# A decoder block's kernel: convolution taps one chunk later, the state space's whole turns rounded by ScalarE, one product by rstd squared, and the last scaling four rows at a time on two engines

## The chip, the cores and the metric

The kernel runs on one core of a Trainium2 chip. The metric is device time in microseconds for one execution, the median of a few runs. Engines are named as the profile names them: PE is TensorE, DVE VectorE, ACT ScalarE, POOL GpSimd, SP the engine that only issues DMAs.

## The reference

One decoder block over 512 tokens of width 2048, batch 1, float32 throughout:

```
proj = rmsnorm(x) @ w_in                      # u, v, gate_b, gate_c (1024 each), merge_a, merge_b (2048 each)
ya   = gelu(s5_scan(u))                       # 64 groups x 64 complex states, a linear recurrence over the tokens
ya   = (ya * sigmoid(ya @ w_glu)) @ w_ssm_out
yb   = (gate_b * causal_dwconv(gate_c * v)) @ w_conv_out        # 3 taps per channel
h    = x + (sigmoid(merge_a) * ya + sigmoid(merge_b) * yb) @ w_o
a    = rmsnorm(h) @ w_up                      # two halves of 5632
h    = h + (gelu(causal_dwconv(a[:5632])) * a[5632:]) @ w_down
out  = rmsnorm(h)                             # mean over channels, times a gain per channel
```

## The kernel before

Channels lie on the 128 partitions, tokens along the free axis. A float32 product is made of three matmuls in a rounded format: each weight chunk and each input is split into a high part and a low part (`hi`, `lo`), and PE runs hi·hi, hi·lo and lo·hi (lines 167 to 169; 1027 to 1029 for `w_up`).

The work is a flat list of *chunks* (128 output channels by 1024 inputs, 24 matmuls of 512 columns). `run` walks it; after the matmuls of chunk i have been written, `after(i)` writes in this order: the split of chunk i+2 (`prep_to`), the loads ahead, one or two pieces of background work (`bg`), the unit's `hooks`, and the unit's `done` if this was its last chunk. Each engine runs its own instructions in the order in which they were written, and waits at semaphores for the others. A chunk has three buffers, so the split of chunk i+2 can start once PE is through chunk i-1.

The split has two forms. For two chunks in three up to the middle of the merge units ACT writes -raw to `lo` (line 145) and raw to `hi` (146), and a DMA on POOL's queue adds raw to `lo` (147), which leaves the low part. For the others ACT writes `hi` (150) and DVE subtracts (129).

In the first stage the chunks are: u (16 chunks), then eight triples of units v, gate_c, gate_b (chunks 16 to 63), then 32 merge units (chunks 64 to 127). Behind them the state space runs as background work, 32 pairs of groups, in pieces called first, second and third: *third* of step n prepares the angles of pair n (`ssm_phase`: a copy to ACT, line 444; on DVE the angle in turns, 449, its rounding to whole turns by adding and subtracting 12582912, line 451, and the difference, 452) and the two matmuls that feed the scan; *first* of step n+1 writes six products on POOL (`ssm_turn`, lines 98 and 490) and half a scan on DVE (lines 98, 478, 479); *second* takes sine and cosine on ACT (`ssm_trig`, 458 to 460) and the other half of a scan. There is one piece a chunk; every fourth merge unit takes two a chunk.

In a triple, `v_done` copies v from PSUM (617) and multiplies it twice by rstd on POOL; `gc_done` multiplies by gate_c on DVE (the zero-padded tile `zp`), and at once applies three taps (`conv3`: line 610 on ACT, 611 and 612 on DVE) and a product by rstd on POOL (`cv`); `gb_done` multiplies by gate_b.

After `w_down`'s first 12 rows of 128 channels the last four rows are computed as eight units of half the tokens (`ends`), so that the first half's norm and stores overlap the second half's matmuls. `dn_done` adds the residual (1156) and squares (859); `out_store` scales a row by its gain and by the norm (1174, DVE, one row of 256 tokens at a time, 32 in all) and stores two rows a DMA, by turns from SP and ACT (1177). After the last matmul: `out_sums(1)`, rows 8 to 15 of the first half, `out_spread(1)`, sixteen rows of the second half. `SHIFT` places the split weights of the `w_down` units, `ends` too, 48 columns further into their buffers.

Of the kernel before, what the change touches and what calls it, by code (L numbers as in the profile page):

```python
# [8 lines left out]
F32 = mybir.dt.float32  # L9
# [3 lines left out]
ALU = mybir.AluOpType  # L13
# [54 lines left out]
def block_kernel(ctx: ExitStack, tc: tile.TileContext, a: dict):  # L68
# [15 lines left out]
    def V(name, i=None):  # L84
        o, w = VEC[name]
        return vec[:, o:o + w] if i is None else vec[:, o + i:o + i + 1]
# [2 lines left out]
    nc.vector.memset(ones, 1.0)  # L89
    halfpi = const.tile([P, 1], F32, tag="halfpi", name="halfpi")  # L90
    nc.vector.memset(halfpi, math.pi / 2)
    warm = const.tile([P, 1], F32, tag="warm", name="warm")
    nc.scalar.activation(warm, halfpi, AF.Copy)
    rstd = const.tile([P, T], F32, tag="rstd", name="rstd")
# [2 lines left out]
    def mul(o, x, y, eng=nc.vector):  # L97
        eng.tensor_tensor(o, x, y, op=ALU.mult)  # L98
# [119 lines left out]
    def add(*units):  # L218
        for u in units:
            flat.extend((u, c) for c in range(len(u.chunks)))  # L220
# [3 lines left out]
    def kd_chunks(w, n):  # L224
        return [(w[2 * n], 8), (w[2 * n + 1], 8)]
# [26 lines left out]
    def norm_spread(big, cols=slice(0, T)):  # L252
        pb = psm.tile([P, T], F32, tag="mm", name="statb")
        nc.tensor.matmul(pb[:, cols], ones, big[:, cols], start=True, stop=True)
        return pb
# [18 lines left out]
    def st(tag, bufs=1, shape=(P, T), dt=F32):  # L274
        return sp.tile(list(shape), dt, tag=tag, name=tag, bufs=bufs)
# [164 lines left out]
    def ssm_phase(p):  # L440

        br = braw.pop(p)
        bs = st("bst", 3, (P, 2, P), F32R)
        nc.scalar.activation(bs, br, AF.Copy)
        nc.vector.tensor_tensor(bs[64:], br[64:], bs[64:].bitcast(F32), op=ALU.subtract)
        bst[p] = bs
        ph, nk = st("ph", 2), st("nk")
        ph3 = ph.rearrange("p (a b) -> p a b", a=16)
        nc.vector.tensor_tensor(ph3, pha[:, p, :].unsqueeze(2).to_broadcast([P, 16, 32]),
                                phb[:, p, :].unsqueeze(1).to_broadcast([P, 16, 32]), op=ALU.add)  # L450
        nc.vector.tensor_scalar(nk, ph, MAGIC, MAGIC, op0=ALU.add, op1=ALU.subtract)
        nc.vector.tensor_tensor(ph, ph, nk, op=ALU.subtract)
        phs[p] = ph

    def ssm_trig(p):
        ph = phs.pop(p)
        t = pairt("cs", 3)
        nc.scalar.activation(t[:, 1], ph, AF.Sin, scale=TURN)
        nc.scalar.activation(t[:, 0], ph, AF.Abs)
        nc.scalar.activation(t[:, 0], t[:, 0], AF.Sin, scale=-TURN, bias=halfpi)  # L460
        cs[p] = t
# [21 lines left out]
    def ssm_turn(p):  # L483
        t, z = cs.pop(p), zz.pop(p)
        x = pairt("xx", 5)
        for j in range(2):
            w = st("pt")
            mul(x[:, j], z[:, j], t[:, 0], nc.gpsimd)
            mul(w, z[:, 1 - j], t[:, 1], nc.gpsimd)
            nc.gpsimd.tensor_tensor(x[:, j], x[:, j], w, op=ALU.add if j else ALU.subtract)  # L490
        xx[p] = x
# [22 lines left out]
    def bg_pieces(n):  # L514

        def ok(p):
            return 0 <= p < NPAIR

        def quad(m):
            return m % 4 == 3 and ok(m)  # L520

        def first():
            if quad(n - 6):
                ssm_y((n - 6) // 4)
            if quad(n - 5):
                ssm_out((n - 5) // 4)
            if ok(n - 3):
                ssm_turn(n - 3)
            if ok(n - 2):
                ssm_scan(n - 2, 0)  # L530

        def second():
            if ok(n - 1):
                ssm_trig(n - 1)
            if ok(n - 2):
                ssm_scan(n - 2, 1)

        def third():
            if quad(n - 4):
                ur_load((n - 4) // 4)  # L540
            if ok(n - 1):
                ssm_bu(n - 1)
            if ok(n):
                ssm_phase(n)
                ssm_load(n + 1)
        return [first, second, third]
# [43 lines left out]

    def u_first():
        nc.vector.tensor_copy(rstd, norm_spread(big[0]))
        for i in range(4):
            mul(uts[i], uts[i], rstd)

# [12 lines left out]
    def conv3(dst, zp, w, b, i, nw):  # L608

        nc.scalar.activation(dst, zp[:, 2:], AF.Identity, scale=V(w, 2 * nw + i), bias=V(b, i))  # L610
        nc.vector.scalar_tensor_tensor(dst, zp[:, 1:T + 1], V(w, nw + i), dst, op0=ALU.mult, op1=ALU.add)
        nc.vector.scalar_tensor_tensor(dst, zp[:, 0:T], V(w, i), dst, op0=ALU.mult, op1=ALU.add)

    def v_done(i):
        def f(ps):
            hold["v"] = st("mt", 2)
            nc.scalar.activation(hold["v"], ps, AF.Copy)
            mul(hold["v"], hold["v"], rstd, nc.gpsimd)
            mul(hold["v"], hold["v"], rstd, nc.gpsimd)
        return f  # L620

    def gc_done(i):
        def f(ps):
            z = zpad[i % 2]
            mul(z[:, 2:], ps, hold["v"])
            hold["cv"] = st("cv", 2)
            conv3(hold["cv"], z, "cw", "cb", i, KS)
            mul(hold["cv"], hold["cv"], rstd, nc.gpsimd)
        return f

    def gb_done(i):
        def f(ps):
            t = hold["cv"]
            mul(t, ps, t)
            later.append(lambda: nc.sync.dma_start(cb_dram[i], t))
        return f
# [13 lines left out]
    for i in range(8):  # L650
        add(Unit(kd_chunks(w_in, 8 + i), xs1, v_done(i), bg=1),
            Unit(kd_chunks(w_in, 24 + i), xs1, gc_done(i), bg=1),
            Unit(kd_chunks(w_in, 16 + i), xs1, gb_done(i), bg=1))
    merges = [Unit(kd_chunks(w_in, 32 + n), xs1, m_done(n), bg=1 + (n % 4 == 0)) for n in range(2 * KD)]
    add(*merges)
    for u, _ in flat[20:]:
# [189 lines left out]
    def hrow(i, cols=slice(0, T)):  # L846
        return ff["H"][i // KS][:, i % KS, cols]
# [5 lines left out]
    def sumsq(i, cols=slice(0, T)):  # L853
        h = hrow(i, cols)
        if i == 0:
            nc.scalar.activation(acc[:, cols], h, AF.Square)
            return
        ff["sq"] = fx("sq", (P, T + 16))[:, :T]
        nc.scalar.activation(ff["sq"][:, cols], h, AF.Square)  # L859
        if i < KD - 1:  # L860
            nc.gpsimd.tensor_tensor(acc[:, cols], acc[:, cols], ff["sq"][:, cols], op=ALU.add)  # L861
# [291 lines left out]
    def dn_done(i, last, cols=slice(0, T)):  # L1153
        def f(ps):
            h = hrow(i, cols)
            nc.vector.tensor_tensor(h, ps[:, cols], h, op=ALU.add)
            if last:
                sumsq(i, cols)
        return f


# [5 lines left out]
    def out_spread(h):  # L1167
        ff["pb"] = norm_spread(ff["big"], HALVES[h])

    def out_store(h, i0, i1):  # L1170
        cols = HALVES[h]
        for i in range(i0, i1):
            x = hrow(i, cols)
            nc.vector.scalar_tensor_tensor(x, x, V("gf", i), ff["pb"][:, cols], op0=ALU.mult, op1=ALU.mult)
            if i % 2:
                x = ff["H"][i // KS][:, i % KS - 1:i % KS + 1, cols]
                (nc.sync if i % 4 == 1 else nc.scalar).dma_start(
                    out[i - 1:i + 1, :, cols].rearrange("a p t -> p a t"), x)

    for b_, (k0, kn) in enumerate(DOWN):  # L1180
        m = 6 if kn == 12 else 8
        last = k0 + kn == KF

        def down(n, **kw):
            return Unit([(a["w_down"][n][:, k * P:(k + m) * P], m) for k in range(k0, k0 + kn, m)],
                        lambda k, k0=k0: xsd(k0 + k), dn_done(n, last, **kw), late=bool(kw), **kw)

        def shifted(u):
            u.off = SHIFT
            return u  # L1190

        dns = [down(n) for n in range(KD - SPLIT if last else KD)]
        if not last:
            k1, n1 = DOWN[b_ + 1]
            if b_ == 0:
                dns[0].hooks[0] = [lambda: [dg_load(k) for k in range(8, 12)]]
            for j in range(n1):
                dns[3 + j].hooks.setdefault(0, []).append(lambda k=k1 + j: dg_split(k))
        add(*map(shifted, dns))
        if last:  # L1200

            ends = [down(n, cols=c) for c in HALVES for n in range(KD - SPLIT, KD)]
            ends[SPLIT].hooks[0] = [lambda: out_sums(0)]
            ends[SPLIT + 1].hooks[0] = [lambda: out_spread(0)]
            ends[SPLIT + 1].post = lambda: out_store(0, 0, 4)
            ends[SPLIT + 2].post = lambda: out_store(0, 4, 8)
            add(*map(shifted, ends))

    run(3, len(flat))

    out_sums(1)
    out_store(0, 8, KD)
    out_spread(1)
    out_store(1, 0, KD)


# [61 lines left out]
```

## Time and profile before

| | us |
|---|---|
| three runs: median (lowest, highest) | 2546.85 (2544.71, 2547.42) |
| the profiled execution, own time | 2549.99 |
| its span, first to last instruction | 2548.2 |
| PE busy in the span | 2497.5 |
| first stage, triples (132.57 to 396.97): DVE busy | 248.02 of 264.40 |
| first stage, merge units (396.97 to 645.85): DVE busy | 239.72 of 248.88 |

The span is read by stage. From 650 us to 2500 us PE is busy without a gap to speak of. What is not matmul at full pace lies in the first 25 us, in the first stage up to about 600 us, and in the last 50 us.

### The profile page before, as it was taken

What the parts mean: (1) busy time and instruction counts of PE and PEld (TensorE: products, weight loads), DVE (VectorE), ACT (ScalarE), POOL (GpSimd) and SP (SyncE); (2) the same over time, 40 slices, a digit from 0 to 9 for tenths busy, and PEclk for the clock granted to TensorE, in tenths of its full rate; (3) what the DMA queues carried; (4) which work ended last, traced back from release to release, by engine and by line L of the source; (5) the groups of instructions that cost most, each with busy time, mean ns of one, the idle gap of its engine ahead of it and who ended that gap; (6) DMA issues with size and microseconds to landing.
All of it is one profiled execution on the core that took longest, in us unless ns stands there. A gap on an engine that the chain in (4) does not pass through costs nothing.

```text
span 2548.2 us, 36443 instructions
## 1 busy us (share of the span) xinstructions
PE 2497.5 (98%) x14616; PEld 2195.8 (86%) x14616; DVE 1711.2 (67%) x1979; ACT 1048.8 (41%) x1331; POOL 559.5 (22%) x431
## 2 busy tenths in 40 slices
PE   8999999999999999999999999999999999999997
PEld 7877777777888888888999999999999988888887
DVE  7799999999323555446777777888787753333335
ACT  5344444444233433334455455555555532222222
POOL 1067767687202121110000000000000000000011
PEclk9999999999999999999999999999999999999999
DMA  5766677777445334444666666676666673434335
GB/s 186 224 165 174 172 187 188 188 190 194 144 147 203 120 132 141 145 142 128 169 174 185 175 167 170 192 190 181 166 177 183 188 254 109 132 108 130 99 94 152
DMA packets 149337, 418.40 MB, mean 164 GB/s; under 512 B 17840, under 2 KB 26160, under 8 KB 149168
## 3 DMA queue, kind: packets, MB, share of 16 engines
q1 hardware_dynamic: 121648, 330.88, 40.8%
q0 software_dynamic: 20448, 74.46, 15.5%
q10 hardware_dynamic: 7072, 10.74, 1.2%
q8 instruction: 114, 1.87, 0.3%
q14 instruction: 55, 0.45, 0.1%
HBM read 300.67 MB, written 40.89 MB: 134 GB/s over the span
## 4 chain that ended last, share of the span: by engine, by line
PE 80%; DMA 5%; DVE 5%; issue 4%; POOL 3%; ACT 2%; SPq 0%; ACTq 0%; DVEq 0%; POOLq 0%
PE mm L169 18%; PE mm L167 18%; PE mm L168 18%; PE sr L1029 9%; PE sr L1027 8%; PE sr L1028 8%; DMA wlo<-wraw 2%; DVE wlo L129 2%; ACT whi L150 1%; DMA wraw<-wraw 1%; POOL pt L98 1%; POOL xx L98 1%; POOL xx L490 1%; PE py L498 1%; DMA th<-ghl 0%
## 5 line engine op out<-in xcount | busy, mean ns | idle before, releaser
L129 DVE TENSOR_TENSOR wlo<-wraw,whi 128x1024 fp32r<-128x1024 f32 (+1 forms) x396 | 479.7, 1211 | 368.8 <-ACT whi L150 368.3
L150 ACT ACTIVATE whi<-wraw 128x1024 fp32r<-128x1024 f32 (+1 forms) x396 | 395.3, 999 | 488.4 <-PE mm L168 391.5
L169 PE MATMUL mm<-xh,wlo 128*128 128x512 f32 x1344 | 530.4, 395 | 23.0 <-DMA wlo<-wraw 20.9
L167 PE MATMUL mm<-xh,whi 128*128 128x512 f32 x1344 | 530.9, 395 | 6.5 <-ACT whi L101 5.7
L168 PE MATMUL mm<-xl,whi 128*128 128x512 f32 x1344 | 528.9, 394 | 0.0
L1029 PE MATMUL sr<-x2h,wlo 128*128 128x256 f32 x1376 | 386.7, 281 | 1.6 <-DVE wlo L129 1.0
L1027 PE MATMUL sr<-x2h,whi 128*128 128x256 f32 x1376 | 384.2, 279 | 0.9 <-ACT whi L150 0.9
L1028 PE MATMUL sr<-x2l,whi 128*128 128x256 f32 x1376 | 383.9, 279 | 0.0
L169 PEld LDWEIGHTS mm<-xh,wlo 128*128 128x128 f32 x1344 | 255.9, 190 | 81.9 <-DMA wlo<-wraw 25.9
L167 PEld LDWEIGHTS mm<-xh,whi 128*128 128x128 f32 x1344 | 255.8, 190 | 67.0 <-issue 6.1
L168 PEld LDWEIGHTS mm<-xl,whi 128*128 128x128 f32 x1344 | 255.8, 190 | 54.7 <-DVE xl L106 0.9
L1029 PEld LDWEIGHTS sr<-x2h,wlo 128*128 128x128 f32 x1376 | 259.7, 189 | 3.9 <-DVE wlo L129 3.4
L1027 PEld LDWEIGHTS sr<-x2h,whi 128*128 128x128 f32 x1376 | 260.1, 189 | 1.1 <-ACT whi L150 1.1
L1028 PEld LDWEIGHTS sr<-x2l,whi 128*128 128x128 f32 x1376 | 260.2, 189 | 0.0
L169 PE MATMUL mm<-x2h,wlo 128*128 128x512 f32 (+1 forms) x528 | 195.4, 370 | 0.8 <-DVE wlo L129 0.8
L167 PE MATMUL mm<-x2h,whi 128*128 128x512 f32 (+1 forms) x528 | 196.1, 371 | 0.0
L168 PE MATMUL mm<-x2l,whi 128*128 128x512 f32 (+1 forms) x528 | 195.2, 370 | 0.0
L1029 PE MATMUL sr<-th,wlo 128*128 128x256 f32 x688 | 192.7, 280 | 1.3 <-DVE wlo L129 1.3
L1027 PE MATMUL sr<-th,whi 128*128 128x256 f32 x688 | 192.4, 280 | 0.0
L1028 PE MATMUL sr<-tl,whi 128*128 128x256 f32 x688 | 192.4, 280 | 0.0
L861 POOL TENSOR_TENSOR acc<-acc,sq 128x512 f32<-128x512 f32 (+1 forms) x31 | 38.5, 1242 | 645.5 <-ACT sq L859 645.5
L129 DVE TENSOR_TENSOR wlo<-r,whi 128x1024 fp32r<-128x1024 f32 x88 | 107.5, 1222 | 47.5 <-ACT whi L150 47.5
(247 smaller groups left out, 4589.2 us busy)
## 6 DMA issues: line engine op xcount, KB each, us to landing
wraw<-in_w_in SPq DMA_DIRECT2D x127, 512.0 KB, 4.3
r<-in_w_up SPq DMA_DIRECT2D x88, 512.0 KB, 6.0
xgb<-in_w_up SPq DMA_DIRECT2D x84, 512.0 KB, 5.3
wraw<-in_w_down SPq DMA_DIRECT2D x104, 384.0 KB, 3.2
wlo<-wraw POOLq DMA_DIRECT2D x56, 512.0 KB, 6.5
wraw<-wraw POOLq DMA_DIRECT2D x43, 512.0 KB, 9.6
wraw<-in_w_o SPq DMA_DIRECT2D x32, 512.0 KB, 3.5
r<-r POOLq DMA_DIRECT2D x22, 512.0 KB, 4.7
```

Of the source, the lines that this page charges most:

```text
L98: eng.tensor_tensor(o, x, y, op=ALU.mult)
L129: nc.vector.tensor_tensor(o, x, y, op=ALU.subtract)
L150: nc.scalar.activation(hi[:, w], raw[:, w], AF.Copy)
L167: nc.tensor.matmul(u.ps[:, u.cols], hi[:, w], xh, start=first, stop=False)
L168: nc.tensor.matmul(u.ps[:, u.cols], hi[:, w], xl, start=False, stop=False)
L169: nc.tensor.matmul(u.ps[:, u.cols], lo[:, w], xh, start=False, stop=last)
L490: nc.gpsimd.tensor_tensor(x[:, j], x[:, j], w, op=ALU.add if j else ALU.subtract)
L498: nc.tensor.matmul(py[32 * q:32 * q + 32, :], cblk[:, p, j, :], xx[p][:, j], start=(j == 0), stop=(j == 1))
L861: nc.gpsimd.tensor_tensor(acc[:, cols], acc[:, cols], ff["sq"][:, cols], op=ALU.add)
L1027: nc.tensor.matmul(ps, hi[:, w], xh, start=(c < 4 and j == 0), stop=False, skip_group_check=c >= 4)
L1028: nc.tensor.matmul(ps, hi[:, w], xl, start=False, stop=False, skip_group_check=c >= 4)
L1029: nc.tensor.matmul(ps, lo[:, w], xh, start=False, stop=j == 7, skip_group_check=c >= 4)
```

## The change

Five edits. (1) `branch_conv` takes the taps and the product by rstd out of `gc_done`; it is a hook of gate_b's first chunk, so it is written one chunk later, behind that chunk's split and background piece. (2) In `ssm_phase` ACT writes the angle plus 12582912 (453 in the new numbering), and the new `ssm_whole`, in *first* of the next step, makes one DVE instruction of subtracting that number and the angle (458); the sign is turned, and the sine's scale with it. (3) `acc`, free by then, takes rstd squared, and v is multiplied once. (4) `dn_done` of the last quarter scales each row by its gain on ACT (1168); `out_store` multiplies four rows by the norm in one instruction (1190) and stores four rows a DMA, from SP and ACT by turns; in the second half the last four rows go first and to POOL, which needs the norm in SBUF (1189, an ACT copy). (5) `ends` are no longer shifted.

```diff
@@ ssm_phase
-        nc.vector.tensor_scalar(nk, ph, MAGIC, MAGIC, op0=ALU.add, op1=ALU.subtract)
-        nc.vector.tensor_tensor(ph, ph, nk, op=ALU.subtract)
-        phs[p] = ph
+        nc.scalar.activation(nk, ph, AF.Identity, bias=magic)
+
+    def ssm_whole(p):
+        ph, nk = phs[p]
+        nc.vector.scalar_tensor_tensor(ph, nk, MAGIC, ph, op0=ALU.subtract, op1=ALU.subtract)
@@ ssm_trig
-        nc.scalar.activation(t[:, 1], ph, AF.Sin, scale=TURN)
+        nc.scalar.activation(t[:, 1], ph, AF.Sin, scale=-TURN)
@@ bg_pieces, first()
                 ssm_turn(n - 3)
+            if ok(n - 1):
+                ssm_whole(n - 1)
             if ok(n - 2):
@@ u_first
+        mul(acc, rstd, rstd)
@@ v_done
-            mul(hold["v"], hold["v"], rstd, nc.gpsimd)
-            mul(hold["v"], hold["v"], rstd, nc.gpsimd)
+            mul(hold["v"], hold["v"], acc, nc.gpsimd)
@@ gc_done
-            hold["cv"] = st("cv", 2)
-            conv3(hold["cv"], z, "cw", "cb", i, KS)
-            mul(hold["cv"], hold["cv"], rstd, nc.gpsimd)
+    def branch_conv(i):
+        hold["cv"] = st("cv", 2)
+        conv3(hold["cv"], zpad[i % 2], "cw", "cb", i, KS)
+        mul(hold["cv"], hold["cv"], rstd, nc.gpsimd)
...
-            Unit(kd_chunks(w_in, 16 + i), xs1, gb_done(i), bg=1))
+            Unit(kd_chunks(w_in, 16 + i), xs1, gb_done(i), bg=1, hooks={0: [lambda i=i: branch_conv(i)]}))
@@ dn_done
                 sumsq(i, cols)
+                nc.scalar.activation(h, h, AF.Copy, scale=V("gf", i))
@@ out_store
-            nc.vector.scalar_tensor_tensor(x, x, V("gf", i), ff["pb"][:, cols], op0=ALU.mult, op1=ALU.mult)
...
+        for i in range(i0, i1, 4):
+            x = ff["H"][i // KS][:, i % KS:i % KS + 4, cols]
+            r = ff["pb"][:, cols]
+            eng = nc.vector
+            if own and i == KD - 4:
+                eng, r = nc.gpsimd, rstd[:, cols]
+                nc.scalar.activation(r, ff["pb"][:, cols], AF.Copy)
+            eng.tensor_tensor(x, x, r.unsqueeze(1).to_broadcast([P, 4, T // 2]), op=ALU.mult)
+            (nc.scalar if i % 8 else nc.sync).dma_start(out[i:i + 4, :, cols].rearrange("a p t -> p a t"), x)
@@ the last units and the end
-            add(*map(shifted, ends))
+            add(*ends)
...
-    out_store(1, 0, KD)
+    out_store(1, KD - 4, KD, True)
+    out_store(1, 0, KD - 4)
```

ACT in one triple, from the end of gate_c to the second chunk after it, before (`wlo` and `whi` are the split of a chunk, `cs` sine and cosine, `cv` the first tap, `bst` the scan's input weights):

```order
L458 ACTIVATE cs<-ph 128x512
L459 ACTIVATE cs<-ph 128x512
L460 ACTIVATE cs<-cs,halfpi 128x512
L610 ACTIVATE cv<-zp_104,vec 128x512
L145 ACTIVATE wlo<-wraw 128x1024
L146 ACTIVATE whi<-wraw 128x1024
L444 ACTIVATE bst<-braw 128x256
L145 ACTIVATE wlo<-wraw 128x1024
L146 ACTIVATE whi<-wraw 128x1024
```

and now:

```order
L463 ACTIVATE cs<-ph 128x512
L464 ACTIVATE cs<-ph 128x512
L465 ACTIVATE cs<-cs,halfpi 128x512
L147 ACTIVATE wlo<-wraw 128x1024
L148 ACTIVATE whi<-wraw 128x1024
L446 ACTIVATE bst<-braw 128x256
L453 ACTIVATE nk<-ph,magic 128x512
L618 ACTIVATE cv<-zp_106,vec 128x512
L147 ACTIVATE wlo<-wraw 128x1024
L148 ACTIVATE whi<-wraw 128x1024
```

The first tap has moved behind one split of the accumulated form, and the rounding `nk` stands ahead of it, behind `bst`.

DVE at the same place, before (`zp` is v times gate_c, `ph` the angle, `zz` and `dt` the scan):

```order
L98 TENSOR_TENSOR zp_103<-mm,mt 128x512
L611 SCALAR_TENSOR_TENSOR cv<-zp_103,vec,cv 128x512
L612 SCALAR_TENSOR_TENSOR cv<-zp_103,vec,cv 128x512
L445 TENSOR_TENSOR bst<-braw,bst 64x256
L449 TENSOR_TENSOR ph<-pha,phb 128x512
L451 TENSOR_SCALAR nk<-ph 128x512
L452 TENSOR_TENSOR ph<-ph,nk 128x512
L98 TENSOR_TENSOR zz<-w_1126,cs 128x512
L98 TENSOR_TENSOR dt_1186<-w_1127,cs 128x512
L478 TENSOR_TENSOR zz<-zz,dt_1186 128x512
```

and now:

```order
L100 TENSOR_TENSOR zp_105<-mm,mt 128x512
L447 TENSOR_TENSOR bst<-braw,bst 64x256
L451 TENSOR_TENSOR ph<-pha,phb 128x512
L619 SCALAR_TENSOR_TENSOR cv<-zp_105,vec,cv 128x512
L620 SCALAR_TENSOR_TENSOR cv<-zp_105,vec,cv 128x512
L458 SCALAR_TENSOR_TENSOR ph<-nk,ph 128x512
L100 TENSOR_TENSOR zz<-w_1123,cs 128x512
L100 TENSOR_TENSOR dt_1188<-w_1124,cs 128x512
L483 TENSOR_TENSOR zz<-zz,dt_1188 128x512
```

The rounding has left DVE, the taps come after the angle, and one instruction on `ph` stands where two were, behind the taps.

ACT at the end of the program, from the last units on, before (`r` and `xgb` are the rows of the output):

```order
L859 ACTIVATE sq<-xgb 128x256
L1177 DMA out_t<-r 128x2x256
L150 ACTIVATE whi<-wraw 128x768 x2
L859 ACTIVATE sq<-xgb 128x256
L1177 DMA out_t<-r 128x2x256
L859 ACTIVATE sq<-xgb 128x256
L241 ACTIVATE ns_22335<-ns_22334 128x2
L1177 DMA out_t<-xgb 128x2x256 x2
```

and now:

```order
L868 ACTIVATE sq<-xgb 128x256
L1168 ACTIVATE xgb<-xgb,vec 128x256
L1191 DMA out_t<-r 128x4x256
L868 ACTIVATE sq<-xgb 128x256
L1168 ACTIVATE xgb<-xgb,vec 128x256
L243 ACTIVATE ns_22342<-ns_22341 128x2
L1191 DMA out_t<-xgb 128x4x256
L1189 ACTIVATE rstd<-statb 128x256
L1191 DMA out_t<-xgb 128x4x256
L1191 DMA out_t<-r 128x4x256
```

A scaling by the gain follows each square, the first store no longer stands ahead of a split, and POOL's copy of the norm stands between two stores.

## Rows read from the trace of the kernel before

**Rows 1.** Busy time by stretch, core 0 (columns in the first line).
```profile
core 0: us, PE busy (x) PEld busy (x) DVE busy (x) ACT busy (x) POOL busy (x), PEclk, DMA share, GB/s
132.57:396.97 264.40, 250.55 (x1086) 200.38 (x1085) 248.02 (x215) 108.63 (x141) 187.42 (x137) 0.97 0.69 175
396.97:645.85 248.88, 239.72 (x1057) 190.40 (x1056) 239.72 (x217) 110.72 (x147) 179.11 (x126) 0.98 0.76 195
1300.00:1315.00 15.00, 15.00 (x131) 14.91 (x130) 11.02 (x14) 8.04 (x10) 0.86 (x1) 1.00 0.65 162
2496.00:2511.00 15.00, 15.00 (x128) 15.00 (x127) 8.56 (x10) 6.69 (x10) 3.40 (x4) 1.00 0.58 161
```

**Rows 2.** Waits of the whole run: total us, times, longest us.
```profile
PE mm L169 <- DMA wlo<-wraw: 20.9, 10, 4.4
ACT cs L458 <- DVE ph L452: 76.0, 19, 8.8
```

**Rows 3.** Timeline of PE: start us, us, instruction, idle before it in brackets.
```profile
173.28 0.62 PE L169 MATMUL mm<-xh,wlo 128*128 128x512 f32 x1 [2.12 <-DMA wlo<-wraw]
```

**Rows 4.** Timeline of ACT, DVE and POOL ahead of that wait.
```profile
164.94 0.81 ACT L610 ACTIVATE cv<-zp,vec 128x512 f32<-128x512 f32 x1 [8.43 <-DVE zp L98]
165.66 1.05 ACT L145 ACTIVATE wlo<-wraw 128x1024 fp32r<-128x1024 f32 x1
...
164.24 0.66 DVE L98 TENSOR_TENSOR zp<-mm,mt 128x512 f32<-128x512 f32 x1
...
161.40 1.84 POOL L490 TENSOR_TENSOR xx<-xx,pt 128x512 f32<-128x512 f32 x1
167.40 1.30 POOL L98 TENSOR_TENSOR cv<-cv,rstd 128x512 f32<-128x512 f32 x1 [4.16 <-DVE cv L612]
168.64 1.76 POOL L147 DMA_DIRECT2D wlo<-wraw  x2
```

**Rows 5.** Line 147, the accumulating DMA of POOL's queue.
```profile
DMA to landing us min/median/max: 4.5/6.5/8.7
```

**Rows 6.** Groups by line and form, 100 to 645 us: busy us, mean ns, idle before.
```profile
L479 DVE TENSOR_TENSOR_SCAN zz<-sm_mag,zz 128x512 f32<-128x512 f32 x64 | 115.5, 1805 | 2.2
L478 DVE TENSOR_TENSOR zz<-zz,dt 128x512 f32<-128x512 f32 x64 | 74.9, 1171 | 2.2
L452 DVE TENSOR_TENSOR ph<-ph,nk 128x512 f32<-128x512 f32 x31 | 49.6, 1599 | 1.1
L451 DVE TENSOR_SCALAR nk<-ph 128x512 f32<-128x512 f32 x31 | 45.6, 1472 | 1.1
```

**Rows 7.** Durations by line (ns, min/median/max).
```profile
L451 DVE TENSOR_SCALAR nk<-ph x32: 426/1389/4000, 94.7 to 618.6; 128x512 f32<-128x512 f32 x32
L452 DVE TENSOR_TENSOR ph<-ph,nk x32: 692/1663/4064, 95.1 to 620.1; 128x512 f32<-128x512 f32 x32
L479 DVE TENSOR_TENSOR_SCAN zz<-sm_mag,zz x64: 1224/2196/2853, 118.3 to 644.7; 128x512 f32<-128x512 f32 x64
L459 ACT ACTIVATE cs<-ph x32: 613/616/618, 105.4 to 622.3; 128x512 f32<-128x512 f32 x32
```

**Rows 8.** Timeline of ACT and DVE in the merge units.
```profile
403.50 1.05 ACT L145 ACTIVATE wlo<-wraw 128x1024 fp32r<-128x1024 f32 x1
...
409.35 1.67 DVE L449 TENSOR_TENSOR ph<-pha,phb 128x512 f32<-128x512 f32 x1
```

**Rows 9.** Last units and tail: PE, ACT and DVE in time.
```profile
2526.83 0.39 PE L169 MATMUL mm<-x2h,wlo 128*128 128x256 f32 x1 [0.49 <-DVE wlo L129]
...
2524.93 1.58 ACT L150 ACTIVATE whi<-wraw 128x768 fp32r<-128x768 f32 x2 [2.45 <-DVE r L1174]
...
2534.82 3.22 DVE L1174 SCALAR_TENSOR_TENSOR xgb<-xgb,vec,statb 128x256 f32<-128x256 f32 x8
```

**Rows 10.** DMA, 2536 to 2547 us: busy tenths in 40 slices, packets.
```profile
DMA  0079999999999999999999999999999999995000
DMA packets 3264, 3.15 MB, mean 286 GB/s; under 512 B 192, under 2 KB 3264, under 8 KB 3264
```

More of the change, by code (lines that the diff above doesn't have):

```diff
@@ L91, in block_kernel @@
     nc.vector.memset(halfpi, math.pi / 2)
+    magic = const.tile([P, 1], F32, tag="magic", name="magic")
+    nc.vector.memset(magic, MAGIC)
     warm = const.tile([P, 1], F32, tag="warm", name="warm")
@@ L446, in ssm_phase @@
         bst[p] = bs
-        ph, nk = st("ph", 2), st("nk")
+        ph, nk = phs[p] = st("ph", 2), st("nk")
         ph3 = ph.rearrange("p (a b) -> p a b", a=16)
@@ L450, in ssm_phase @@
                                 phb[:, p, :].unsqueeze(1).to_broadcast([P, 16, 32]), op=ALU.add)
-        nc.vector.tensor_scalar(nk, ph, MAGIC, MAGIC, op0=ALU.add, op1=ALU.subtract)
-        nc.vector.tensor_tensor(ph, ph, nk, op=ALU.subtract)
-        phs[p] = ph
+        nc.scalar.activation(nk, ph, AF.Identity, bias=magic)
+    def ssm_whole(p):
+        ph, nk = phs[p]
+        nc.vector.scalar_tensor_tensor(ph, nk, MAGIC, ph, op0=ALU.subtract, op1=ALU.subtract)
     def ssm_trig(p):
-        ph = phs.pop(p)
+        ph, _ = phs.pop(p)
         t = pairt("cs", 3)
-        nc.scalar.activation(t[:, 1], ph, AF.Sin, scale=TURN)
+        nc.scalar.activation(t[:, 1], ph, AF.Sin, scale=-TURN)
         nc.scalar.activation(t[:, 0], ph, AF.Abs)
@@ L1168, in out_spread, with out_store @@
         ff["pb"] = norm_spread(ff["big"], HALVES[h])
-    def out_store(h, i0, i1):
+    def out_store(h, i0, i1, own=False):
         cols = HALVES[h]
-        for i in range(i0, i1):
-            x = hrow(i, cols)
-            nc.vector.scalar_tensor_tensor(x, x, V("gf", i), ff["pb"][:, cols], op0=ALU.mult, op1=ALU.mult)
[L1175 to L1178, printed above, removed]
+        for i in range(i0, i1, 4):
[7 more added lines that the diff above has]
+            (nc.scalar if i % 8 else nc.sync).dma_start(out[i:i + 4, :, cols].rearrange("a p t -> p a t"), x)
     for b_, (k0, kn) in enumerate(DOWN):
```

## The prediction

> **What bounds the kernel now.** I read busy time by stretch first, then PE's waits, then the timeline behind one of them. From 650 us to about 2500 us PE has no gap that is worth anything, so nothing that the other engines save there counts. What can be won lies in the first stage, where the triples run 13.85 us and the merge units 9.16 us without a matmul, and where the granted clock averages 0.97 and 0.98 of 2.4 GHz [rows 1]: the mean is below one because the clock stands at 1.2 GHz for some time after a wait. In time that is 250.55 x 0.03 = 7.5 us and 239.72 x 0.02 = 4.8 us. So the first stage can give back at most 13.85 + 7.5 + 9.16 + 4.8 = 35.3 us, of which 21.4 in the triples, and no sum of saved instructions may exceed that.
>
> Nearly all the idle time is ten waits for the accumulated low weights, 20.9 us together [rows 2]. One of them shows the cause [rows 3, 4]. PE waits 2.12 us until 173.28, so it wanted the chunk at 171.16. The accumulating DMA was issued on POOL's queue at 168.64 and landed some 4.6 us later, the quickest that such a DMA takes [rows 5]: what is late is its issue. It stood behind `cv`, POOL's product, which waited 4.16 us for the taps on DVE; and the split itself stood on ACT behind the first tap, which waited 8.43 us for DVE's `zp`. DVE in turn is busy for 248.02 of 264.40 us [rows 1]. So DVE is the bound of the triples, by way of two queues that stand behind it.
>
> DVE is that busy partly because it waits for POOL inside its instructions. The rounding (451) takes 0.43 us at the least and 1.39 at the median, the difference (452) 0.69 and 1.66, the scan (479) 1.22 and 2.20: about 0.97 more each, while ACT's 459 always takes 0.61 to 0.62 [rows 7]. With the means of [rows 6], and 0.69 as the least for 478, a two-input product of the same form, that is 31 x (1.47 - 0.43) + 31 x (1.60 - 0.69) + 64 x (1.17 - 0.69) + 64 x (1.81 - 1.22) = 129 us, against 137 + 126 POOL instructions in the two stretches [rows 1]: 0.49 us of DVE for each.
>
> **Taps a chunk later (1).** In the example the split would no longer stand behind the first tap, nor its DMA behind `cv`. POOL was through its turn at 161.40 + 1.84 = 163.24 and ACT was waiting from 156.5 on, so the DMA can go at about 163.3, 5.3 us earlier than 168.64; at the median 6.5 us [rows 5] it lands at 169.8, before 171.16, and only the slowest (8.7) misses, by 0.8. That wait goes. The next chunk's DMA now stands behind `cv`: the taps come after DVE's `bst` and angle, 1.67 us [rows 8] and a little, so `cv` starts at about 169.4 instead of 167.40 and ends at 170.7 (1.30 long), and the DMA lands at 175.2 (4.5), 177.2 (6.5) or 179.4 (8.7). PE wants it one chunk after the first, and a chunk is 24 matmuls of 250.55 x 0.97 / 1086 = 0.224 us at full clock, 5.4 us, or some 5.75 with what the clock loses: at 176.5 to 176.9. So 0 to 0.7 us of wait remains by the median and 2.9 by the worst. A triple lasts 264.40 / 7 = 37.8 us, and without idle or lost clock (264.40 - 21.4) / 7 = 34.7. Per triple I get from nothing, if the second wait takes the first's place, to -3.1: 0 to -21.4 in all. I take half, -11, since one of two chunks is freed with room to spare and the other is on the edge.
>
> **Rounding on ACT (2).** DVE loses 451 and keeps one instruction with two inputs in SBUF, of the kind of 452. It saves 0.43 us a step at the least, 1.39 at the median [rows 7], 13 to 43 us over 31 steps. The new instruction takes 0.69 alone by 452, and 1.66 when it meets POOL. ACT's `nk` takes 0.62 by 459; 32 of them are 20 us on an engine that is busy for 108.63 of 264.40 [rows 1]. The new cost is a wait of DVE for `nk`. In the triples the two taps stand between the angle and 458 and cover it. In the merge units nothing but what first writes ahead of it on DVE does: up to 0.62 us and a hand-over for some 17 steps, about +11, with both scans of the pair and the next split's subtraction queued behind. ACT in turn waits at `nk` for DVE's angle, and the next split and `m_done`'s copy stand behind that. Before, ACT had started a split at 403.50 while the angle ended at 409.35 + 1.67 = 411.02 [rows 8]. Against it stand at least 0.43 x 17 = 7 us of DVE saved there. I take 0 for the merge units, with +8 and -12 (of the 14.0 to be had) as ends.
>
> The 129 us show that DVE and POOL hold each other up, and whichever instruction of DVE meets POOL's pays. If the lost time belongs to POOL's product, and not to 451, it moves to the next instruction with operands in SBUF (458, 478, 479), and only 0.43 of the 1.39 is saved. The Trainium skill, "SBUF — State Buffer", section "SBUF: two separate sides", says the same as a rule: VectorE and GpSimd share a pair of ports as an exclusive lock, held for a whole instruction, and the other fully blocks. By that rule the saving is 13 us and not 43; the trace agrees as far as the 0.97 us goes, and cannot show where the wait would move.
>
> **One product by rstd squared (3).** One POOL product of 1.30 us a triple goes, by `cv` [rows 4], with it 0.49 us of DVE (at most 0.97): 7 x 0.49 = 3.4 us inside the -11. The multiplication that makes `acc` costs DVE some 0.7 us once, before the triples, beside PE's first chunks; 0.
>
> **Last units and tail (4, 5).** PE's wait of 0.49 us at 2526.83 stands behind a split that ACT began late, 2.45 us behind DVE's row, since a store stood ahead of it on ACT [rows 9]; the first store is SP's now, so -0.5. Unshifted, the last units may run at the closer pitch: 128 matmuls of 256 columns in 15 us there, 131 at 1300 us where other buffers feed the same form [rows 1], that is 0.1172 against 0.1145 us. For 288 matmuls it is -0.8 if the place of the weights makes the difference and 0 if not; I take -0.4. Behind the last matmul DVE scales 24 rows in 3 x 3.22 = 9.7 us (eight rows take 3.22) [rows 9]. Four rows in one instruction cost less, by the form of 452 (512 columns in 0.69, so 1024 in some 1.2) 5 x 1.2 = 6.0, with POOL's group of some 2.4 us beside it. But from 2537 to 2546 the 16 DMA engines are full, 3.15 MB in some 33 slices of 0.275 us [rows 10]. The bytes do not change and the first store cannot come much earlier, since it now waits for four rows: 0, between -2.5 (a shorter end of the last store) and +0.5. By the Trainium skill, "DMA: Bandwidth & Descriptors", "Specifications", a core's HBM limit is about 358 GB/s, and these 3.15 MB would be an estimated 8.8 us, so the tail could give 0.3 us at most; the trace moves 3.15 MB in 9.1 us, 346 GB/s.
>
> The gain now takes a pass of ACT for each of the last quarter's rows of 256 tokens, 12 or so, under matmuls, where ACT is busy for 6.69 of 15 us [rows 1]: 0.
>
> **Sum.** -11 + 0 - 0.9 + 0 = -12. The profiled execution took 2549.99 us, 3.1 over the median of 2546.85; 2538 on its scale, 2534.5 on the median's, which is what is forecast.
>
> **The rivals.** (A) Everything in the first stage goes: -35.3 - 0.9 gives 2510.5. For it speaks that the ten waits share one cause, DVE's lateness, and that ACT waits for DVE's angle for another 76.0 us [rows 2], a wait that gets shorter with every us of DVE; against it, that a merge unit has none of the taps and little of its DVE time goes.
>
> (B) No change, about 2546. The wait for POOL only moves, the wait for `nk` takes the 0.43 that is left, and in the triples the second accumulated chunk waits for what the first did. For it: 0.97 us more on every kind of instruction alike [rows 7]. Against it: the split and its DMA leave two queues whatever DVE does. The rule of the Trainium skill's "SBUF — State Buffer", section "SBUF: two separate sides", carried through, gives this case.
>
> (C) Slower: ACT held at `nk`. Where a merge unit takes two pieces a chunk, the split behind `nk` starts when DVE's angle is done, at 411.02 + 0.62 and not at 403.50. Its DMA goes at 412.7 and lands at 417.2 to 419.2 [rows 5]; PE wants it two chunks after the split could start, 403.50 + 2 x 5.75 = 415.0. That is a wait of 2.2 to 4.2, say 3.2, and the clock with it, 12.3 / 10 = 1.2: 4.4 in each of five such places, +22, less the 12: 2557. It decides where the angle ends more than some 4 us behind the time that the split could start. Against it: DVE is relieved of 451 in just these places, and of its lag of 7.5 us part goes.
>
> That the change doesn't do what it says is unlikely: the order of ACT and DVE moves as described.
>
> **How the numbers follow.** About 0.2% (5.1 us) is what a measurement of this kernel can tell from no change: faster is below 2541.8, slower above 2551.9. The forecast, 2534.5, has 0.58, with 2518 to 2541 for its own range (triples 0 to -21, merge units +8 to -12, not all at one end). A has 0.16, B 0.17 (2541 to 2551), C 0.09. Faster: 0.58 + 0.16 = 0.74; same 0.17; slower 0.09. The range reaches from A's 2510, losing a third of A, to 2548, losing C and a third of B: 0.05 + 0.09 + 0.06 = 0.20.
>
> **What would show it.** In the triples PE's waits for the accumulated weights should be gone or below 0.7 us, the clock there 0.98 or more, POOL's DMA ahead of `cv`. A second wait of 2 us behind `cv` in each triple would refute (1). ACT should show a wait of `nk` for DVE; if it is followed by PE's waits in the merge units, C holds. If 458, 478 and 479 get longer by what 451 was over 0.43, the saving of (2) is 13 us and not 43. In the last units 131 matmuls in 15 us would confirm (5), 128 refute it; the tail's DMA should stay full for as long. Slower last units or a longer tail alone would upset 1 us of the sum, longer merge units most of it.

## The result: slower, and not where the prediction looked

The changed kernel takes 2561.73 us (2558.71 to 2565.99, six runs) against 2545.45 (2541.55 to 2547.42) before, 16.3 us slower in the medians where 12 us faster were forecast; the ratio is 1.0067, interval 1.0054 to 1.0080. The profiled executions' spans are 2559.9 and 2548.2 us. Cut at the matmuls of each stage, from one profiled execution each (us). "kh" is the stage whose input lies mostly in the buffer `kh` (the products with `w_conv_out` and `w_ssm_out`, and the one with `w_glu` between them); "between" is the product with `w_o` and what stands beside it; "w_up" is called sr in the expectations below. One chunk between the merge units and kh, 5.4 us in both, stands in no column.

| | triples | merge units | kh | between | w_up | w_down | tail |
|---|---|---|---|---|---|---|---|
| before | 297.95 | 376.13 | 217.15 | 199.02 | 851.46 | 484.72 | 17.33 |
| after | 278.50 | 387.25 | 222.28 | 199.58 | 858.68 | 491.09 | 17.15 |
| difference | -19.5 | +11.1 | +5.1 | +0.6 | +7.2 | +6.4 | -0.2 |

The differences add up to 10.7 us and not to 16.3, chiefly because the execution of before that was profiled, 2549.99 us, lies 4.5 us over its median.

The triples gave almost all of the 21.4 us that could be had there. The merge units gave back more than half of it. And the stages behind them, of which the prediction's first paragraph said that nothing there counts, are 19.3 us longer (5.1 + 0.6 + 7.2 + 6.4), without a wait of PE to show for it.

First the triples, PE's waits from 99.9 to 378.5 us in the changed kernel (total us, times, longest); [rows 2] is the whole of before:

```profile
PE mm L171 <- DMA wlo<-wraw: 1.9, 2, 1.2
```

The merge units, 378.5 to 766 us; the whole run of before had ten such waits, 20.9 us, and four of these, 7.1 us, lie in its merge units:

```profile
PE mm L171 <- DMA wlo<-wraw: 17.6, 8, 4.4
```

The new waits of ACT and DVE on each other, of the whole run; ACT's 76.0 us ahead of sine and cosine [rows 2] are gone for them:

```profile
ACT nk L453 <- DVE ph L451: 140.0, 32, 6.9
DVE ph L458 <- ACT nk L453: 15.0, 19, 0.8
```

The stretches that answer to [rows 1]: the first is now without idle time to speak of and at the full clock, the second is not.

```profile
132.57:396.97 264.40, 262.41 (x1170) 210.91 (x1169) 238.39 (x215) 126.72 (x168) 201.43 (x138) 1.00 0.72 185
396.97:645.85 248.88, 230.50 (x1011) 181.19 (x1010) 222.74 (x187) 112.40 (x152) 180.31 (x124) 0.98 0.69 185
```

Behind 650 us no wait explains anything. Here the same matmuls stand further apart. The instructions that read `kh`, before (how many, min/median/max in ns, first and last start):

```profile
L167 PE MATMUL mm<-kh,whi x256: 389/389/389, 778.5 to 995.5; 128*128 128x512 f32 x128
```

and in the changed kernel:

```profile
L169 PE MATMUL mm<-kh,whi x256: 395/396/397, 771.1 to 993.2; 128*128 128x512 f32 x128
```

256 instructions, no gap, 217.0 us from first to last before and 222.1 now. Every one is 6 to 8 ns longer; start to start, most matmuls of `kh` lie 0.231 to 0.235 us apart, and before 0.226 to 0.227. The clock does not differ: PEclk is 1.00 in both there. The instructions that read `xl`, from 700 us on, kept their median of 389 ns. So what changed is a property of pairs of buffers, not of the engine.

### The profile page after: what moved, and what is told of

Its sections match the earlier page's. It is cut to its first block, busy times and chain, and to the rows that moved or that the text cites. A ratio compares the mean times of both kernels' runs of the same rounds, so it can differ in the third digit from the quotient of the medians.

```text
span 2559.9 us, 36427 instructions
## 1 busy us (share of the span) xinstructions
PE 2513.8 (98%) x14616; PEld 2197.5 (86%) x14616; DVE 1673.2 (65%) x1924; ACT 1080.8 (42%) x1384; POOL 563.2 (22%) x424
## 4 chain that ended last, share of the span: by engine, by line
PE 86%; DVE 4%; issue 4%; POOL 3%; DMA 2%; ACT 1%; SPq 0%; DVEq 0%; ACTq 0%; POOLq 0%
PE mm L171 18%; PE mm L169 18%; PE mm L170 18%; PE sr L1038 11%; PE sr L1036 11%; PE sr L1037 11%; DMA wlo<-wraw 1%; DVE zz L483 1%; POOL xx L100 1%; POOL pt L100 1%; POOL xx L495 1%; DVE wlo L131 1%; DMA wraw<-wraw 0%; PE py L503 0%; DVE zz L100 0%
## 5 line engine op out<-in xcount | busy, mean ns | idle before, releaser
L131 DVE TENSOR_TENSOR wlo<-wraw,whi 128x1024 fp32r<-128x1024 f32 (+1 forms) x396 | 488.1, 1233 | 384.8 <-ACT whi L152 384.4
L171 PE MATMUL mm<-xh,wlo 128*128 128x512 f32 x1344 | 528.0, 393 | 19.6 <-DMA wlo<-wraw 19.5
```

Source lines behind the costliest of these rows:

```text
L131: nc.vector.tensor_tensor(o, x, y, op=ALU.subtract)
L171: nc.tensor.matmul(u.ps[:, u.cols], lo[:, w], xh, start=False, stop=last)
```

## The line that was not priced

The diff under "The change" does not show where the number 12582912 is kept. It is a new constant of one column.

```diff
     nc.vector.memset(halfpi, math.pi / 2)
+    magic = const.tile([P, 1], F32, tag="magic", name="magic")
+    nc.vector.memset(magic, MAGIC)
     warm = const.tile([P, 1], F32, tag="warm", name="warm")
```

Its memset costs 0.06 us, and the prediction passed over it. But in the two built programs everything allocated behind it on the left side of memory stands 32 bytes further: the `whi` buffers at 35552, 39904 and 44256 instead of 35520, 39872 and 44224 (bytes in a partition), `wlo`, `xh`, `th` likewise. `kh` (133056) and `x2h` (161664) are allocated from the right and stayed. The products that slowed down are those whose input stayed while their weights moved. In `w_up`, matmuls of 256 columns, those that read `x2h` lie 0.1197 us apart on average instead of 0.1173 (4128 of them), and those that read `th`, which moved along, 0.1154 instead of 0.1167.

## Experiments

Stage lengths of every kernel (us, one profiled execution each), and its time against the kernel before with the 95% interval, from all runs. "Pad" kernels differ by unused tiles alone. Before and its four pads run the same instructions; their triples lie between 293.6 and 298.0 us and their merge units between 375.0 and 376.9, so a difference of some 4 us in the triples says nothing by itself.

| kernel | triples | merge units | kh | w_up | w_down | ratio |
|---|---|---|---|---|---|---|
| before | 297.95 | 376.13 | 217.15 | 851.46 | 484.72 | 1 |
| after | 278.50 | 387.25 | 222.28 | 858.68 | 491.09 | 1.0067 (1.0054 to 1.0080) |
| before_pad32 | 297.33 | 375.97 | 222.28 | 859.56 | 491.59 | 1.0087 (1.0073 to 1.0101) |
| before_pad64 | 296.15 | 374.97 | 222.27 | 861.26 | 491.05 | 1.0079 (1.0066 to 1.0091) |
| before_pad128 | 297.88 | 376.88 | 222.25 | 855.64 | 491.39 | 1.0062 (1.0048 to 1.0075) |
| before_pad256 | 293.61 | 375.17 | 217.15 | 851.84 | 484.18 | 0.9997 (0.9987 to 1.0006) |
| after_pad64 | 277.47 | 386.74 | 222.27 | 861.40 | 491.66 | 1.0064 (1.0052 to 1.0077) |
| after_edge | 280.31 | 388.43 | 217.15 | 854.34 | 481.98 | 0.9972 (0.9961 to 0.9982) |
| taps_only | 277.72 | 377.49 | 217.15 | 852.99 | 483.70 | 0.9925 (0.9913 to 0.9938) |
| round_edge | 280.06 | 387.35 | 217.15 | 852.08 | 484.15 | 0.9983 (0.9974 to 0.9992) |
| vprod_only | 290.25 | 375.59 | 217.15 | 851.84 | 484.55 | 0.9989 (0.9980 to 0.9997) |
| no_round | 276.36 | 374.34 | 217.15 | 852.09 | 481.99 | 0.9905 (0.9891 to 0.9918) |
| whole_late | 282.75 | 388.68 | 217.15 | 853.14 | 482.53 | 0.9986 (0.9977 to 0.9995) |
| nk_behind_split | 274.73 | 372.93 | 217.15 | 853.24 | 483.00 | 0.9898 (0.9885 to 0.9912) |

**Is it the place of the weights?** The kernel before with one unused tile:

```diff
+    const.tile([P, 1], F32, tag="pad0", name="pad0")
     warm = const.tile([P, 1], F32, tag="warm", name="warm")
```

> The kernel before with one unused constant tile of one column, which moves the weight buffers 32 bytes up and leaves the inputs of the later products where they are. Theory P (place): in the changed kernel the tile for the number 12582912 did the same, and matmuls whose weights and inputs lie 32 bytes apart are slower: the three stretches behind the merge units (kh, sr, w_down) get 5.1 + 7.2 + 6.4 = 18.7 us longer, 2545.5 + 18.7 = 2564, with 512-column matmuls of kh at 0.231 to 0.235 us instead of 0.227. Rival S (schedule): the slower pace comes from the changed instructions; an unused tile does nothing, 2545 within 3.

Measured: 2570.53 against 2548.44 us, 22 us slower, kh 222.28 us. No instruction differs. P holds against S: the schedule has no part in the slower pace.

```profile
L168 PE MATMUL mm<-kh,whi x256: 395/396/397, 778.4 to 1000.5; 128*128 128x512 f32 x128
```

**Which places are bad?** Two such tiles, and the changed kernel with a second one behind `magic`, move the weights by 64 bytes:

> Two unused tiles, so the weight buffers move by 64 bytes. Theory P: what counts is the place within 64 bytes, which is as before: 2545 within 3, kh at 0.227 us. Rival M (any move of the buffers against the inputs costs): 2564 as with 32 bytes. Rival S: 2545.

> The changed kernel with one unused tile behind the new constant, so that the weight buffers stand 64 bytes from their old place and not 32. Theory P: the 18.7 us go, 2561.7 - 18.7 = 2543, a little under before. Rivals S and M: 2562 as the changed kernel.

Both stayed slow, 2568.56 and 2564.18 us. So P's detail was wrong: the place within 64 bytes does not decide. That left "any move costs" (M), or a longer period. Divided by 256, the old addresses of `whi` all leave 192, and so does `kh`; `x2h` leaves 128, and there `SHIFT` moves the weights by 192 bytes, which leaves 128 too. Hence P2, tried with four and eight unused tiles:

> The kernel before, weight buffers 128 bytes further. Theory P2: weights and inputs that stand at the same place within 256 bytes run at 0.227 us for 512 columns (before: 35520 and 133056 both leave 192 when divided by 256), all others at 0.231 to 0.235: kh 222 us and about 2567 as with 32 and 64. Rival P3 (the place within 128 bytes): kh 217.2 and 2548.

> The kernel before, weight buffers 256 bytes further. Theory P2: the same place within 256 bytes again, so kh 217.2 us at 0.227 and 2548 within 4. Rival M (any move costs, as 32 and 64 did): 222 us and 2567.

128 bytes: kh 222.25, 2565.36 us. 256 bytes: kh 217.15, 2547.58 against 2548.79 us. The rows of before_pad128

```profile
L171 PE MATMUL mm<-kh,whi x256: 391/394/399, 778.6 to 1000.6; 128*128 128x512 f32 x128
```

and of before_pad256:

```profile
L175 PE MATMUL mm<-kh,whi x256: 388/389/390, 772.8 to 989.7; 128*128 128x512 f32 x128
```

M and P3 fall, and P2 stands for the matmuls of 512 columns: the same place within 256 bytes is fast, 32, 64 and 128 bytes off are slow. Why the place matters no run shows, and other distances were not tried. For the 256-column matmuls P2 is no rule. The last units, 288 of them, take 37.3 us before, where weights and inputs agree within 256 bytes by `SHIFT`, and that is the slowest: 36.9 us at 32 bytes off (before_pad32), 36.3 and 35.8 at 64 (before_pad64 and, unshifted, after_edge), 36.4 at 96 (the changed kernel, unshifted), 36.9 and 37.1 at 128 (after_pad64, before_pad128).

**The change without the move.** The number goes into a spare tile that both kernels hold at the right end:

```diff
-    edge.tile([P, 8], F32, tag="edge", name="edge")
+    spare = edge.tile([P, 8], F32, tag="edge", name="edge")
...
-    magic = const.tile([P, 1], F32, tag="magic", name="magic")
+    magic = spare[:, 0:1]
```

> The changed kernel with the number 12582912 in a column of the spare tile at the right end of memory that both kernels hold, so that no buffer moves; all five edits stay. If the move of the weight buffers, by 32 bytes or 64, is what makes the later products slow, the stretches kh, sr and w_down take 217.2, about 852 and about 482 us again and 18.7 us go: 16.3 - 18.7 = 2.4 under the kernel before, about 2545. If the changed instructions slow PE, it is as slow as the changed kernel: 16 over before.

Measured: 2542.35 against 2549.29 us, 7 us faster, kh 217.15. The place of one constant turns the five edits from 7 us faster to 16 slower, some 23 us in the medians.

**Which edit does what.** The rounding taken back, the other edits kept; no constant, so nothing moves:

```diff
-        nc.scalar.activation(nk, ph, AF.Identity, bias=magic)
+        nc.vector.tensor_scalar(nk, ph, MAGIC, MAGIC, op0=ALU.add, op1=ALU.subtract)
+        nc.vector.tensor_tensor(ph, ph, nk, op=ALU.subtract)
+        phs[p] = ph
...
-            if ok(n - 1):
-                ssm_whole(n - 1)
```

> The changed kernel without the rounding on ScalarE (lines 451 and 452 on VectorE as before, no new constant, so nothing moves); the other four edits stay. Theory C (ScalarE held at nk lengthens the merge units by 11.1 us): P's 18.7 and C's 11.1 go, the triples keep their 19.5: 2561.7 - 29.8 = 2532. Rival D (the triples got faster because VectorE was relieved of the rounding): the merge units return to 376 us but the triples lose 10 or more of the 19.5: 2542 or above.

Measured: 2524.98 us, 23.5 under before and 17 under after_edge: merge units 374.34 against 388.43 us; that the triples are 3.9 us shorter too is within what two executions differ by. Theory C. Each of three edits alone, on the kernel before:

> The kernel before with the taps a chunk later alone. If the taps' place is what freed the triples: 298.0 us of triples become 280 to 284 (of the 21.6 us that four edits took, 1.3 us of POOL in each of eight triples and 0.5 of VectorE are the product by rstd squared), 2547 - 16 = 2531. If the product is what counts: 290 or more, 2540.

> The kernel before with the rounding on ScalarE alone, its number in the spare tile, nothing moved. Theory C (ScalarE held at nk, the split behind it): the merge units get some 12 us longer, as 387 against 374 us with and without it among the other edits; the triples within 5 us of before: 2547 + 12 = 2559. Rival D (VectorE relieved helps): merge units no longer and triples some 10 shorter, 2537.

> The kernel before with v multiplied once, by rstd squared, alone. If a product less on GpSimd gives VectorE 0.5 us a triple as the prediction had it: 298 us of triples become 293 to 296, 2545. If it frees the queue on which the accumulating DMAs stand: 285 to 290, 2537.

The taps alone: triples -20.2, 2530.87 us, 18.4 under before. The product alone: 2546.63 us, 2.2 under before, which fits the first expectation and not the second. Its triples are 7.7 us shorter, but the two executions that were profiled, 2549.99 and 2542.05 us, lie 7.9 apart where the medians lie 2.2 apart: most of the 7.7 is the executions' difference and not the product's. The rounding alone: triples -17.9 and merge units +11.2, 2544.91 (4.4 under). There C was right on the merge units and D on the triples, and both on the total wrong. The gains in the triples do not add up: -20.2 for the taps and -17.9 for the rounding alone, -21.6 for taps and product together, -17.6 with the rounding as well. After one of the first two there is little left to take.

**Whose wait lengthens the merge units?** In the changed kernel two waits are new there, ACT's for the angle and DVE's for `nk`. `whole_late` takes DVE's away:

```diff
-            if ok(n - 1):
-                ssm_whole(n - 1)
...
             if ok(n - 1):
+                ssm_whole(n - 1)
                 ssm_trig(n - 1)
```

> after_edge with VectorE's one instruction on nk (458) written in the next background piece, right ahead of sine and cosine, so that VectorE no longer waits for ScalarE's nk (15.0 us in 19 waits in the changed kernel), while ScalarE still waits at nk for VectorE's angle. Theory C: the merge units stay at 385 to 389 us, 2545. Rival E (it is VectorE's own wait that costs the merge units): they return to 374 to 377 us, 2533.

Merge units 388.68, 2545.69 us: C, not E. But the edit gives ACT another wait, so by itself it does not decide. ACT waits for the angle and then for the whole turns:

```profile
ACT cs L463 <- DVE ph L458: 150.9, 32, 8.5
ACT nk L453 <- DVE ph L451: 67.9, 32, 4.7
```

`nk_behind_split` keeps both instructions and lets ACT split the next chunk first:

```diff
         prep_to(i + 3, u.late)
+        while held:
+            held.pop()()
...
-        nc.scalar.activation(nk, ph, AF.Identity, bias=magic)
+        held.append(lambda: nc.scalar.activation(nk, ph, AF.Identity, bias=magic))
...
             if ok(n - 1):
+                while held:
+                    held.pop()()
                 ssm_whole(n - 1)
```

> after_edge with ScalarE's nk written behind the next chunk's split (or right ahead of 458, where that comes first), so that ScalarE waits for the angle with the split behind it and not ahead. Theory C (nk holds the split, the split holds the accumulating DMA, and that the two turns behind it on GpSimd's queue): the merge units go from 388 to 375 to 379 us, 2542.4 - 11 = 2531. Rival F (the merge units are long because VectorE's and ScalarE's instructions on the angle now wait for each other): they stay at 385 or more.

Measured: merge units 372.93 us, 2522.75 against 2548.79 us, 26 us faster than before and the fastest kernel of the study. This decides against E and F: DVE waits for `nk` longer than in the changed kernel (15.0 us there), ACT still waits for the angle (57.0 us in 13 waits, against 140.0 in 32), and the merge units are the shortest of all.

```profile
DVE ph L461 <- ACT nk L456: 34.3, 27, 3.5
```

The chain can be read in the timelines. In the changed kernel (start us, us, idle before in brackets), where the merge units begin at 378.46, ACT:

```profile
389.88 0.72 ACT L453 ACTIVATE nk<-ph,magic 128x512 f32<-128x512 f32 x1 [6.81 <-DVE ph L451]
390.50 1.05 ACT L147 ACTIVATE wlo<-wraw 128x1024 fp32r<-128x1024 f32 x1
```

POOL and PE:

```profile
391.85 0.88 POOL L149 DMA_DIRECT2D wlo<-wraw  x1 [4.27 <-ACT wlo L147]
392.46 1.60 POOL L100 TENSOR_TENSOR xx<-zz,cs 128x512 f32<-128x512 f32 x1
...
400.53 1.63 POOL L495 TENSOR_TENSOR xx<-xx,pt 128x512 f32<-128x512 f32 x1
402.10 0.88 POOL L149 DMA_DIRECT2D wlo<-wraw  x1
...
406.66 0.50 PE L171 MATMUL mm<-xh,wlo 128*128 128x512 f32 x1 [4.41 <-DMA wlo<-wraw]
```

and in nk_behind_split, where they begin at 373.45, ACT:

```profile
379.09 1.07 ACT L148 ACTIVATE wlo<-wraw 128x1024 fp32r<-128x1024 f32 x1 [0.85 <-PE mm L172]
...
386.68 0.73 ACT L456 ACTIVATE nk<-ph,edge 128x512 f32<-128x512 f32 x1 [5.58 <-DVE ph L454]
```

POOL and PE:

```profile
380.46 0.88 POOL L150 DMA_DIRECT2D wlo<-wraw  x1 [0.47 <-ACT wlo L148]
...
392.66 0.88 POOL L150 DMA_DIRECT2D wlo<-wraw  x1 [0.18 <-issue]
...
397.25 0.50 PE L172 MATMUL mm<-xh,wlo 128*128 128x512 f32 x1 [0.51 <-DMA wlo<-wraw]
```

ACT waits about as long for the angle at this place in both. Ahead of the split, the wait makes the split 6.4 us later (12.0 us after the start of the merge units against 5.6). The split delays its DMA, the DMA delays the turn that is queued behind it on POOL (one turn, six products, where the expectation speaks of two), and the turn delays the next accumulating DMA: 23.6 us after the start against 19.2, 4.4 us. PE then waits 4.41 instead of 0.51. Of the eight waits of the changed kernel's merge units (17.6 us) three, 8.3 us, are of this kind. In the other five, 9.3 us, PE waits for the DMA of the very split that stood behind `nk`, as rival C had it.

## Why the prediction was wrong

**What bounds the kernel now: half right.** The ten waits, their cause and the cap of 21.4 us for the triples were right: 19.5 us came. The step that failed is the sentence that from 650 us on nothing counts. It holds for saved engine time, and the sum took it for the kernel as a whole: it priced instructions and queues, and the place of the weights for the last units alone (0.4 us, under (4, 5)). Its cases held no rival in which matmuls get slower. From the stages this costs 18.7 us (5.1 + 7.2 + 6.4), from the medians with and without the move some 23, more than the whole forecast. The diff had it: an allocation ahead of the weight buffers, in a kernel that already carries a constant, `SHIFT`, whose only use is to place weights.

**Taps a chunk later (1): right, undersized.** -20.2 us in the triples alone, 18.4 in the medians, where -11 was taken; the end of the range was -21.4, worked out for seven of the eight triples. The second accumulated chunk, which the working left on the edge, waited 1.2 us at most in the changed kernel.

**Rounding on ACT (2): wrong for the merge units.** The step took 0 there, with -12 and +8 as ends; it is +11.1, and +14.1 between no_round and after_edge, outside the range. Rival C named the place and the mechanism, ACT held at `nk`, and gave 2.2 to 4.2 us for each of five waits; there are eight, 17.6 us together and 4.4 at the longest, where before had four of 7.1 us. C's +22 was twice what came. It got 0.09, since the working credited DVE with being relieved in just these places. The relief was small. These groups, 100 to 645 us of the changed kernel (busy us, mean ns), answer [rows 6]:

```profile
L484 DVE TENSOR_TENSOR_SCAN zz<-sm_mag,zz 128x512 f32<-128x512 f32 x64 | 137.9, 2155 | 2.2
L483 DVE TENSOR_TENSOR zz<-zz,dt 128x512 f32<-128x512 f32 x64 | 112.2, 1753 | 2.2
...
L458 DVE SCALAR_TENSOR_TENSOR ph<-nk,ph 128x512 f32<-128x512 f32 x32 | 24.8, 774 | 15.4 <-ACT nk L453 15.0
```

Lines 451 and 452 of before were 45.6 + 49.6 = 95.2 us, 458 is 24.8: 70.4 saved. But 478 went from 74.9 to 112.2 (483 now) and the scan from 115.5 to 137.9, together 59.7 us more, and 15.0 us of waiting for `nk` are new. In part that is the taps' doing. No_round and after_edge differ in the rounding alone, and there it is 67.7 us for 451 and 452 against 24.7 for 458, 43.0 saved, and 42.0 more in 478 and the scan; the angle (449) gets 15.8 us shorter. So most of the time that DVE lost in 451 and 452 moved to the instructions that are left, as the second argument under (2) had it. Over the two stretches shown above DVE is busy for 461.1 us instead of 487.7, 26.6 less and not 70, and stands still for 15.0 of these. The rule of the Trainium skill, "SBUF — State Buffer", section "SBUF: two separate sides", that one of the two engines holds the shared ports for a whole instruction while the other blocks, fits this row better than a cost tied to line 451.

**One product (3): about right.** Alone it gives 2.2 us in the medians, 0.8 to 5.1 by the interval, where 3.4 was taken. Whether that is DVE's time or the shorter queue ahead of POOL's DMA was not separated.

**Last units and tail (4, 5): the sum about right, by luck.** The 288 matmuls of the last units take 36.4 us from first to last in the changed kernel and 35.8 with nothing moved, 37.3 before: -0.9 and -1.6 against a sum of -0.9. The -0.5 for PE's wait did not come: its waits on DVE's split there are 0.8 us before, 0.7 in the changed kernel and 0.8 in after_edge. The pitch gave more than the -0.4 taken for it (130 matmuls in 15 us from 2496 us on in after_edge, 128 in [rows 1]), and in the changed kernel the new constant took part of it back. The 16 DMA engines are as full as in [rows 10], 2548 to 2559 us:

```profile
DMA  0006999999999958999999999999999999999600
```

and the tail is 17.15 us against 17.33: nothing, as forecast.

**The chances.** Faster had 0.74. Without the new constant's move the forecast's sign was right (0.9972) and its size, 12 us, still too large, by the merge units. With it, what the triples gain is outweighed.

## What to carry to other kernels

Price what a change allocates, not only what it executes: an unused tile of one column made this kernel 22 us slower, so a new constant belongs in memory that is already there, or where it moves nothing that PE reads. When a rounding or any other small step goes to another engine, look at what that engine has queued behind it: here the same instruction, written behind the split instead of ahead of it, is worth some 19 us (ratios to before of 0.9898 and 0.9972). Time that an engine loses to another need not vanish with the instruction in whose row it stands: here 42.0 of 43.0 us came back in other rows. And a stage's length from one execution is not yet an effect: set it beside the medians.

## What the runs showed that was not expected

Matmuls of 512 columns run at 0.226 to 0.227 us when weights and input stand at the same place within 256 bytes, and at 0.233 us on average when they are 32, 64 or 128 bytes apart (mostly 0.231 to 0.235 at 32, 0.228 to 0.238 at 128); for `kh` as a whole this is 2.4% (222.28 against 217.15 us). Those of 256 columns depend on the place too, but by another rule, which stays open: the last units are slowest where the places agree. The move by 256 bytes alone changed nothing that can be measured (0.9997, 0.9987 to 1.0006).
